# The keep factors of stick-breaking attention: a tensor_scalar on VectorE becomes an activation on ScalarE

## The chip, the core and the metric

The kernel runs on one core of a Trainium2 chip. A core has five engines that work side by side and wait for each other through semaphores: TensorE (PE, with its weight loads shown as PEld), VectorE (DVE), ScalarE (ACT), GpSimd (POOL) and SyncE (SP), which here issues the DMAs. Each engine takes its instructions in the order of its own queue. The metric is the device time of one execution in microseconds; several executions give a median.

## What is computed

A decoder trunk of two layers over 1024 tokens of width 1024, in float32. Each layer has three token mixers side by side (stick-breaking attention with 4 heads, latent attention with 4 heads, RWKV-7 with 8 heads), an output projection and a gated feed-forward part with a short convolution. What matters here is stick-breaking attention. For a query t and the positions s < t:

```python
z = einsum('bhqd,bhkd->bhqk', qb, k) * scale
past = kpos[None, :] < qpos[:, None]
log_keep = where(past, log_sigmoid(-z), 0.0)
log_later = cumsum(log_keep, axis=3, reverse=True) - log_keep
w = where(past, exp(log_sigmoid(z) + log_later), 0.0)
out = einsum('bhqk,bhkd->bhqd', w, v)
```

With T = tanh(z/2) the sigmoid of z is (1 + T)/2, and the factor 1 - sigmoid(z), the share of the stick that position s leaves over, is 0.5 - 0.5 T. So the weight of s is (1 + T_s)/2 times the product of the keep factors of all later positions. On the diagonal and behind it T is set to -1, which makes the weight 0 and the keep factor 1.

## The kernel before

Projections, RWKV and the feed-forward part make up most of the time, and in them PE is nearly always busy. The attention stage comes once per layer, at 541 to 700 us and at 2041 to 2200 us of the profiled span. In it four streams are woven together: two of latent attention (`mla`, one per head of a pair) and two of stick-breaking attention (`stick`). Each stream goes through two pairs of heads (`pr` 0 and 1) and in each through 8 blocks of 128 query rows. In pair 0 the blocks grow from 128 to 1024 key columns, in pair 1 they shrink again. So there are 32 stick-breaking blocks per layer and 64 in all, eight of each of eight lengths.

One stick-breaking block (`stick_block`, then `stick_post`) goes through these steps:

- PE multiplies queries by keys in one or two pieces of up to 512 columns (L388, L389).
- ACT takes the tangent of each piece from PSUM into the tile `be`, called `mexp` in the trace (L390).
- POOL sets the part of the last 128 columns on and above the diagonal to -1 (`affine_select`, L396).
- DVE makes the keep factors `kp` of columns 1 and up (L397), in one of three buffers called LA, T and pd in the trace.
- DVE runs the product of the keep factors from the right (a scan, L399) and multiplies by 1 + T (L400).
- PE transposes the weights in blocks of 128 (L339), ACT copies them to SBUF (L340), PE multiplies by V (L323), ACT scales the result (L418), and SP stores it.

The latent-attention streams use the same engines: DVE takes maxima (L562) and small statistics (L564, L566, L573, L576, L577), ACT the exponentials (L567, L575), DVE scales them (L580, L582). Near the end of the stage the weights of the output projection are split in two parts (L200 on ACT, L201 on DVE).

No order is written out by hand here. Semaphores are put in by the language's planner, which also orders each engine's instructions at build time, by priorities that start from the program's order and by its own estimate of when operands are ready. The engines then keep that order: an instruction whose operand is late holds up all that stand behind it on its engine.

Of the kernel before, what the change touches and what calls it, by code (L numbers as in the profile page):

```python
# [11 lines left out]
AF = mybir.ActivationFunctionType  # L12
ALU = mybir.AluOpType
# [56 lines left out]
class Body:  # L70
# [322 lines left out]
    def stick_post(self, be, kp, i, LL, nb, n, V, hp, pr, wp):  # L393
        nc = self.nc
        dg = be[:, i * P : LL]
        nc.gpsimd.affine_select(out=dg, in_=dg, pattern=[[-1, P]], base=0, channel_multiplier=1, compare_op=ALU.is_gt, fill=-1.0)  # L396
        nc.vector.tensor_scalar(kp[:, : LL - 1], be[:, 1:LL], -0.5, 0.5, op0=ALU.mult, op1=ALU.add)  # L397
        kv = kp[:, : LL - 1][:, ::-1]
        nc.vector.tensor_tensor_scan(kv, kv, self.ones.to_broadcast([P, LL - 1]), 1.0, op0=ALU.mult, op1=ALU.mult)  # L399
        nc.vector.scalar_tensor_tensor(be[:, :LL], be[:, :LL], 1.0, kp[:, :LL], op0=ALU.add, op1=ALU.mult)  # L400
        wt = self.w_transpose(self.wt4[:, n % 6], be, nb, "pa")
        self.pair(("s", pr, i), wt, hp, nb, V, self.mixd[pr], i, wp, "pa", 0.5)
# [855 lines left out]
```

## Time and profile before

| | |
|---|---|
| median of three executions | 3023.79 us (3023.44 to 3026.31) |
| the profiled execution | 3025.69 us |
| its span, first to last instruction | 3024.0 us |
| PE busy | 2913.1 us, 96% |
| PEld busy | 2322.0 us, 77% |
| DVE busy | 1727.8 us, 57% |
| ACT busy | 1074.8 us, 36% |
| POOL busy | 230.8 us, 8% |
| mean granted TensorE clock | 0.989 |

The busy times are unions of instructions of one engine within the span. A share over the whole span mixes stages in which different engines set the pace. A wait in the profile is idle time of an engine just before an instruction, put down to the instruction whose end released it.

### The profile page before, as it was taken

The numbers are of one execution on the slowest core, as the hardware profiler recorded it, in microseconds if no ns is written. First come the engines' busy times: TensorE is split into PE (matmuls) and PEld (weight loads), VectorE is DVE, ScalarE is ACT, GpSimd is POOL, SyncE is SP. The second block draws the span as 40 slices with busy tenths as digits, with TensorE's granted clock in tenths as the row PEclk, the third lists the DMA queues.
The fourth block names the chain that finished last, engine by engine and source line by source line (L and its number), as shares of the span: only waits on it lengthen the run. The fifth ranks groups of instructions, "written<-read, shape, count | busy, mean of one in ns | idle before, by whom it ended". The sixth has DMA issues, their size and how long they took to land.

```text
span 3024.0 us, 41845 instructions
## 1 busy us (share of the span) xinstructions
PE 2913.1 (96%) x16572; PEld 2322.0 (77%) x16572; DVE 1727.8 (57%) x2857; ACT 1074.8 (36%) x1833; POOL 230.8 (8%) x308
## 2 busy tenths in 40 slices
PE   8999999889999999999999999999899999999998
PEld 6777777667888888888877777776678888888887
DVE  4568665886544444344645677568965443434437
ACT  5454454762211112121254644457612111212120
POOL 0001122030000000000000011210300000000000
PEclk9999999999999999999999999999999999999999
DMA  4353666324411111111124446562244111111111
GB/s 135 91 157 102 209 193 203 92 82 137 167 56 42 42 43 55 49 56 49 63 77 125 127 133 207 177 213 66 90 145 163 42 42 42 56 49 55 50 49 56
DMA packets 338260, 301.78 MB, mean 100 GB/s; under 512 B 24200, under 2 KB 302992, under 8 KB 338064
## 3 DMA queue, kind: packets, MB, share of 16 engines
q1 hardware_dynamic: 338064, 299.11, 32.6%
q8 instruction: 131, 2.15, 0.3%
q14 instruction: 65, 0.53, 0.1%
HBM read 208.87 MB, written 90.18 MB: 99 GB/s over the span
## 4 chain that ended last, share of the span: by engine, by line
PE 76%; DVE 10%; issue 8%; ACT 3%; DMA 3%; POOL 1%; SPq 0%; POOLq 0%; DVEq 0%; ACTq 0%
PE psmm L207 16%; PE psmm L206 16%; PE psmm L205 16%; PE psps L205 5%; PE psps L206 5%; PE psps L207 5%; PE pspa L848 2%; DVE pd L731 1%; PE pspi L792 1%; PE psmt L216 1%; DMA LA<-xxd 1%; DVE T L732 1%; PE pspa L684 1%; ACT pd L726 0%; DVE mexp L400 0%
## 5 line engine op out<-in xcount | busy, mean ns | idle before, releaser
L207 PE MATMUL psmm<-xTh,wlo 128*128 128x512 f32 x2144 | 849.1, 396 | 0.0
L205 PE MATMUL psmm<-xTh,whi 128*128 128x512 f32 x2144 | 847.0, 395 | 0.0
L206 PE MATMUL psmm<-xTl,whi 128*128 128x512 f32 x2144 | 846.8, 395 | 0.0
L200 ACT CAST whi<-raw 128x1024 fp32r<-128x1024 f32 x152 | 160.0, 1053 | 1062.1 <-PE psmm L206 1048.6
L205 PEld LDWEIGHTS psmm<-xTh,whi 128*128 128x128 f32 x2144 | 404.0, 189 | 88.6 <-issue 6.1
L206 PEld LDWEIGHTS psmm<-xTl,whi 128*128 128x128 f32 x2144 | 404.2, 189 | 87.9 <-issue 4.6
L207 PEld LDWEIGHTS psmm<-xTh,wlo 128*128 128x128 f32 x2144 | 404.2, 189 | 87.6 <-issue 4.2
L201 DVE TENSOR_TENSOR wlo<-raw,whi 128x1024 fp32r<-128x1024 f32 x152 | 185.6, 1221 | 456.7 <-ACT whi L200 440.4
L1060 DVE TENSOR_TENSOR y<-y,psps 128x512 f32<-128x512 f32 x288 | 196.5, 687 | 171.1 <-PE psps L207 171.0
L205 PE MATMUL psps<-wdh,hh 128*128 128x512 f32 x672 | 266.7, 397 | 0.0
L206 PE MATMUL psps<-wdl,hh 128*128 128x512 f32 x672 | 262.9, 391 | 0.0
L207 PE MATMUL psps<-wdh,hl 128*128 128x512 f32 x672 | 259.6, 391 | 0.0
L205 PEld LDWEIGHTS psps<-wdh,hh 128*128 128x128 f32 x672 | 126.1, 188 | 36.8 <-ACT hh L200 5.9
L923 POOL TENSOR_TENSOR lsm<-lsm,small 128x1 f32<-128x1 f32 x32 | 29.3, 915 | 1629.9 <-DVE lsm L922 1629.9
L207 PEld LDWEIGHTS psps<-wdh,hl 128*128 128x128 f32 x672 | 126.2, 188 | 26.9
L206 PEld LDWEIGHTS psps<-wdl,hh 128*128 128x128 f32 x672 | 126.2, 188 | 25.4
L1035 DVE TENSOR_TENSOR cv<-cv,psmm 128x1024 f32<-128x1024 f32 x44 | 53.8, 1222 | 136.6 <-PE psmm L207 131.7
L201 DVE TENSOR_TENSOR wdl<-raw,wdh 128x1024 fp32r<-128x1024 f32 x42 | 51.5, 1226 | 88.2 <-ACT wdh L200 88.2
L1030 ACT ACTIVATE cv<-cv 128x1024 f32<-128x1024 f32 x44 | 46.7, 1061 | 115.8 <-DVE cv L1029 115.8
L848 PE MATMUL pspa<-RBl,PSl 128*128 128x128 f32 x512 | 72.0, 286 | 11.1 <-ACT QC L851 5.3
L848 PEld LDWEIGHTS pspa<-RBl,PSl 128*128 128x128 f32 x512 | 64.6, 195 | 19.3 <-ACT QC L851 8.3
L206 PE MATMUL psmm<-wol,whi 128*128 128x512 f32 x192 | 76.6, 399 | 1.6 <-DVE wol L201 1.6
(444 smaller groups left out, 4504.7 us busy)
## 6 DMA issues: line engine op xcount, KB each, us to landing
raw<-in_ffn_w_up_dram SPq DMA_DIRECT2D x88, 512.0 KB
raw<-in_w_in_dram SPq DMA_DIRECT2D x44, 512.0 KB
raw<-in_ffn_w_down_dram SPq DMA_DIRECT2D x44, 512.0 KB
rbd<-RB SPq DMA_DIRECT2D x64, 256.0 KB
PSl<-psd SPq DMA_DIRECT2D x32, 512.0 KB
RBl<-rbd SPq DMA_DIRECT2D x32, 512.0 KB
psd<-Vz SPq DMA_DIRECT2D x64, 128.0 KB
xxd<-X SPq DMA_DIRECT2D x64, 128.0 KB
```

Of the source, the lines that this page charges most:

```text
L200: self.nc.scalar.copy(hi, src)
L201: (eng or self.nc.vector).tensor_tensor(lo, src, hi.bitcast(F32), op=ALU.subtract)
L205: mm(out, lh, rh, start=start, stop=False)
L206: mm(out, lh, rl, start=False, stop=False)
L207: mm(out, ll, rh, start=False, stop=stop)
L216: nc.tensor.transpose(pt[:, k * P : k * P + P], xt[:, kk * P : kk * P + P], self.ident)
L684: ms.append(nc.tensor.matmul(pAs[h][:, cc * P : cc * P + P], flat(BK[hr, 2 * g + cc // 2, cc % 2]), AR[hr, :, 2 * g + cc // 2, cc % 2, :], ...
L731: mul = lambda o, x, y: nc.vector.tensor_tensor(o, x, y, op=ALU.mult)
L848: nc.tensor.matmul(pQ[:, f, e, :], PSh[:, f, h, e, :], RBh[:, f, h, e, :], start=True, stop=True)
L1030: nc.scalar.activation(cv, cv, AF.Gelu)
L1035: nc.vector.tensor_tensor(cv, cv, pg, op=ALU.mult)
L1060: nc.vector.tensor_tensor(y[:, i, hs], y[:, i, hs], ps, op=ALU.add)
```

## The change

The keep factors are made by ACT instead of DVE. The input, the output and the arithmetic (times -0.5, plus 0.5) are the same, and so is the place in the program: behind the clearing of the diagonal by POOL and ahead of the scan on DVE. The scan now waits for ACT instead of following an instruction of its own engine, and ACT now waits for POOL.

```diff
         dg = be[:, i * P : LL]
         nc.gpsimd.affine_select(out=dg, in_=dg, pattern=[[-1, P]], base=0, channel_multiplier=1, compare_op=ALU.is_gt, fill=-1.0)
-        nc.vector.tensor_scalar(kp[:, : LL - 1], be[:, 1:LL], -0.5, 0.5, op0=ALU.mult, op1=ALU.add)
+        nc.scalar.activation(kp[:, : LL - 1], be[:, 1:LL], AF.Copy, scale=-0.5, bias=0.5)
         kv = kp[:, : LL - 1][:, ::-1]
         nc.vector.tensor_tensor_scan(kv, kv, self.ones.to_broadcast([P, LL - 1]), 1.0, op0=ALU.mult, op1=ALU.mult)
```

## Rows read from the trace of the kernel before

**Rows 1.** The page, part 1: busy time of each engine over the span.

```profile
PE 2913.1 (96%) x16572; PEld 2322.0 (77%) x16572; DVE 1727.8 (57%) x2857; ACT 1074.8 (36%) x1833; POOL 230.8 (8%) x308
```

**Rows 2.** Busy by window: us; PE, PEld, DVE, ACT, POOL; clock, DMA share, GB/s.

```profile
541.00:590.00 49.00, 43.31 (x330) 33.33 (x330) 46.26 (x111) 38.57 (x105) 3.97 (x11) 1.00 0.33 90
590.00:632.00 42.00, 35.51 (x294) 27.85 (x293) 34.61 (x65) 28.41 (x73) 17.39 (x20) 0.94 0.15 42
632.00:690.00 58.00, 48.46 (x397) 36.43 (x395) 55.21 (x82) 38.63 (x90) 11.17 (x17) 0.97 0.28 91
...
2134.00:2193.00 59.00, 53.07 (x422) 39.39 (x420) 54.59 (x89) 39.44 (x93) 13.54 (x20) 0.99 0.32 95
```

**Rows 3.** Waits of PE, 537 to 690 and 2040 to 2197: us, times, longest.

```profile
PE pspa L339 <- DVE mexp L400: 8.3, 12, 1.5
PE psav L339 <- DVE mexp L580: 3.6, 7, 0.8
PE pspa L339 <- DVE mst L566: 3.5, 3, 2.1
...
PE psav L339 <- DVE mexp L580: 5.1, 6, 2.7
PE pspa L339 <- DVE mst L566: 2.6, 2, 2.3
PE pspa L339 <- DVE mexp L400: 2.2, 5, 0.8
```

**Rows 4.** Busy time by window, instructions of L397 alone (window, length, DVE busy).

```profile
541.00:590.00 49.00, 3.90 (x11) 1.00 0.33 90
590.00:632.00 42.00, 2.62 (x5) 0.94 0.15 42
632.00:690.00 58.00, 7.79 (x15) 0.97 0.28 91
690.00:700.00 10.00, 0.44 (x2) 0.84 0.45 125
...
2090.00:2134.00 44.00, 3.57 (x5) 0.90 0.11 34
2134.00:2193.00 59.00, 7.44 (x16) 0.99 0.32 95
```

**Rows 5.** Line L397, whole span: ns min/median/max, and idle before it.

```profile
L397 DVE TENSOR_SCALAR LA<-mexp x21: 197/479/694, 549.0 to 2191.7; 128x255 f32<-128x255 f32 x3, 128x383 f32<-128x383 f32 x3, 128x639 f32<-128x639 f32 x3, 128x767 f32<-128x767 f32 x3
...
  POOL mexp L396: 8.8, 12
```

**Rows 6.** Timeline around one cleared diagonal: start us, us, engine, line.

```profile
647.85 1.07 ACT L340 COPY Aa<-pspa 128x512 f32<-128x512 f32 x2
648.03 0.35 POOL L396 TENSOR_SCALAR_AFFINE_SELECT mexp<-mexp 128x128 f32<-128x128 f32 x1 [9.69 <-ACT mexp L390]
648.41 0.63 DVE L397 TENSOR_SCALAR T<-mexp 128x895 f32<-128x895 f32 x1 [0.18 <-POOL mexp L396]
649.08 2.02 DVE L399 TENSOR_TENSOR_SCAN T<-T,small 128x895 f32<-128x895 f32 x1
```

**Rows 7.** Lines L1030, L885, L418, L567 on ACT: ns min/median/max.

```profile
L1030 ACT ACTIVATE cv<-cv x44: 1060/1061/1062, 813.7 to 2965.8; 128x1024 f32<-128x1024 f32 x44
L885 ACT ACTIVATE yq<-ys x32: 415/417/423, 381.0 to 2024.6; 128x256 f32<-128x256 f32 x32
L418 ACT ACTIVATE avo<-pspa x32: 265/278/309, 551.3 to 2196.4; 128x128 f32<-128x128 f32 x32
L567 ACT ACT_TABLE_LOAD  x2: 1283/1283/1283, 517.4 to 2019.4; - x2
```

**Rows 8.** Timeline of DVE in stretch C of layer 0.

```profile
661.23 0.94 DVE L400 SCALAR_TENSOR_TENSOR mexp<-mexp,LA 128x768 f32<-128x768 f32 x1
...
662.16 0.55 DVE L397 TENSOR_SCALAR T<-mexp 128x767 f32<-128x767 f32 x1
...
662.83 1.74 DVE L399 TENSOR_TENSOR_SCAN T<-T,small 128x767 f32<-128x767 f32 x1
```

## Prediction

> **What bounds the kernel now.** I read the page first. TensorE (PE) is busy 96% of a span of 3024.0 us, VectorE (DVE) 57%, ScalarE (ACT) 36% [rows 1]. These are averages over stages with different limits, and the changed line runs in one stage only, the attention, once per layer. So I cut that stage out of the busy-by-window view and split each layer's copy in three: A, the first pair of heads (541 to 590 and 2041 to 2090 us), B, the turn to the second pair (590 to 632, 2090 to 2134), and C, the second pair to the end (632 to 690, 2134 to 2193) [rows 2]. The reader should compare the columns in one line. In A DVE is busy 46.3 of 49 us, PE 43.3, ACT 38.6 (A and B of layer 1 repeat those of layer 0, so only one row of each stands); in C of layer 0 it is DVE 55.2 of 58, PE 48.5, ACT 38.6; in B nobody is above 85%. So in A and C DVE is the fullest engine, at 93 to 95%, and ACT has 30% left. In B, PE, DVE and ACT take turns waiting.
>
> Whether a full DVE is also what PE waits for is a second question, answered by the waits of PE in the two stages. The three largest in layer 0 are all on DVE, 8.3 + 3.6 + 3.5 = 15.4 us, in layer 1 again, 5.1 + 2.6 + 2.2 = 9.9 us [rows 3]. Together 25.3 us: about what DVE's lateness costs PE, and a ceiling for what any relief of DVE can bring, since the work of PE stays.
>
> **What is removed.** L397 (x -> 0.5 - 0.5x, DVE) runs 64 times: 3.90 + 2.62 + 7.79 us in A, B and C of layer 0 and 0.44 us for two behind them, the same 3.9 + 3.57 + 7.44 in layer 1, in all 29.6 us [rows 4]. One takes from 0.197 us at 127 columns to 0.694 at 1023, left alone [rows 5].
>
> **What is added.** Before has no such ACT instruction, so I price it by the nearest ACTIVATEs from SBUF to SBUF with immediate or no operands: 1.061 us at 128x1024 (L1030) and 0.417 us at 128x256 (L885) [rows 7]. The line through them is 0.202 us + 0.839 ns per column. Eight of each of eight lengths, 127 to 1023, are 64 instructions and 36,800 columns: 12.9 + 30.9 = 43.8 us, 21.9 per layer. Bounds: an ACTIVATE on 128x128 from PSUM takes 0.28 us (L418) where my line says 0.31, so 2 us less is possible; the form with two operands per partition is not used, so I see no reason for more. Copies and scaled ACTIVATEs (L340, L418) run between tangents and exponentials now, and the stage has just one table load per layer (x2, 1283 ns [rows 7]), so no table load is added.
>
> The Trainium skill ("ScalarE: Activation LUTs", Rules for kernel authors) says to do additions and multiplications on VectorE and not on ScalarE. The rows agree on the single instruction: 0.69 us on DVE against about 1.06 on ACT for the longest. By that rule alone the change would lose; it is the third rival below.
>
> **What is moved: the wait for the cleared diagonal.** L397 waits for GpSimd's (POOL's) L396, which waits for the tangent L390. Before, DVE stands at this wait. It really idled there only 12 times of 64, 8.8 us in all [rows 5]; the other 52 times it came late, from other work, and the diagonal was long cleared. For those 52 the ACT version can finish before DVE wants to scan, and the DVE time simply drops out: at 662.16 L397 runs right between a product (661.23, 0.94 us) and a scan (662.83) [rows 8]. For the 12 it is the opposite. At 648.03 the diagonal is cleared in 0.35 us, L397 starts 0.03 us later and the scan follows at 649.08 [rows 6]. On ACT the same 895 columns take 0.202 + 0.751 = 0.95 us instead of 0.63, so +0.32 us; and ACT is then inside two copies that began at 647.85 and take 1.07 us, to 648.92, which is 0.54 us past the clearing [rows 6]. So such a block's scan starts 0.32 to 0.86 us later; I take 0.6. No DMA and no SP queue is passed; on POOL nothing moves. But ACT is in order: behind each new instruction stand copies of transposed weights (L340, PE's next operand), exponentials L567 (DVE's reciprocals wait for them) and tangents of the next block. Where POOL is late, all of these wait with it.
>
> **The sum, by stretch.**
> A: DVE goes from 46.3 to 42.4 us. ACT gets 11 instructions of 127 to 767 columns (4,597 in all): 2.2 + 3.9 = 6.1 us, and goes from 38.6 to 44.7 of 49. ACT becomes the fullest engine. If the stretch keeps today's 2.7 us of idle on its fullest engine, it takes 47.4: -1.6 per layer. If the longer ACT run lies wholly in the chain, +2.2 per layer (6.1 - 3.9). I take 0; bounds -3.2 and +4.4 for both layers.
> B: four of the twelve waits lie here (606, 621, 2109, 2121 us): 4 x 0.6 = +2.4. The six others give 6.2 - 2.6 = 3.6 us back to a DVE that is 82% busy, so I count half, -1.8. Sum +0.6; bounds -3.6 and +3.4.
> C: layer 0: DVE 55.2 - 7.8 = 47.4, PE 48.5, ACT 38.6 plus 15 instructions of 255 to 1023 columns (9,969 in all: 3.0 + 8.4 = 11.4 us) = 50.0. The fullest engine goes from 55.2 to 50.0. With the old 2.8 us of idle the stretch takes 52.8, -5.2; with twice that, since three engines are then within 3 us of each other and six of the twelve waits lie in the two C's, 55.6, -2.4. Layer 1: PE's 53.1 is the floor; with DVE's old idle of 4.4 us it takes 57.5, -1.5, with 2.8 us 55.9, -3.1. Both: -3.9 to -8.3. I take -5.0, nearer the small end, because the waits moved to ACT come on top.
> Sum: 0 + 0.6 - 5.0 = -4.4 us. The profiled execution took 3025.7 us, 1.7 of it outside the span, and lies 1.9 us above the median of the runs, 3023.8. I set the change against the median: 3023.8 - 4.4 = **3019.4 us**. Everything outside the two stages (2706 of 3024 us) should be as before, apart from small shifts of order at their edges.
>
> **Rivals.**
> 1. Full relief. For it: PE's largest waits are on DVE, and 52 of 64 factors are not urgent. Then PE wins back half of its 25.3 us of waits on DVE, -12.7 us: 3011. Against it: PE, DVE and ACT would all be at 85 to 90%, and ACT feeds PE too.
> 2. Nothing passes. ACT takes DVE's place as the late engine in A, and in C PE's in-order transposes keep the pace: 3022 to 3026. For it: ACT at 44.7 of 49 in A. Against: C has room on ACT.
> 3. Slower: ACT's queue becomes the bound. Place: A, and the twelve blocks where the diagonal is only just cleared. Price: +4.4 in A, and 12 x 0.6 = 7.2 for the late scans, with no relief used: +11.6, 3035. It decides from the point where ACT, not DVE, is what PE's transposes and score products wait for; ACT's 6.1 us more in A must then displace copies rather than fill its 10.4 us of idle. For it: each factor is 1.5 times as long on ACT, and ACT's idle pieces in A are short. Against: its free time there is larger than what is added.
> 4. The change does not do what it says: the planner places the new instruction late on ACT, or orders PE otherwise, and the stage moves by some us either way.
>
> **How the numbers follow.** A measurement of this kernel tells about 0.2%, 6 us, from no change. Forecast (-10 to +1): 0.40, of which 0.16 lies beyond -6. Rival 1: 0.20, all faster. Rival 2: 0.15, of which 0.02 slower. Rival 3: 0.23, of which 0.03 stays within 6 us. Rival 4: 0.02, half faster, half slower. Faster 0.16 + 0.20 + 0.01 = 0.37; same 0.24 + 0.13 + 0.03 = 0.40; slower 0.02 + 0.20 + 0.01 = 0.23. The range runs from 3006 (rival 1 with two thirds of the ceiling) to 3034 (most of rival 3). The likeliest case alone: 3014 to 3025.
>
> **What would show it.** Right: L397 on ACT at about 0.31 to 1.06 us, 43 to 44 us in all; DVE busy 14 to 15 us less per layer; PE's waits on DVE's L400 and L580 shorter; C of layer 0 shorter by some 3 us, A unchanged; no new table load. Rival 3: ACT idle before L397 <- POOL well over 8.8 us, and PE's top waits on L340, L567 or L390. Rival 1: both C's shorter by 4 us or more and A shorter too. I would be wrong above all if a different order on PE moved the stage by more than the terms above.

## The result and the profile after

The changed kernel takes 3040.67 us (median of four runs, 3037.40 to 3046.96), the kernel before on the same chip 3024.61 (3023.44 to 3026.31): a ratio of 1.0055, interval 1.0038 to 1.0073. It is slower by 16 us, where the forecast was 4.4 us faster and the range ended at 3034. The profiled execution took 3046.96 us with a span of 3045.2, so it lies 6.3 us above the median; the table of its span is read with that in mind.

The page of the changed kernel, part 1, beside [rows 1]:

```profile
PE 2923.0 (96%) x16572; PEld 2331.3 (77%) x16572; DVE 1706.8 (56%) x2793; ACT 1111.0 (36%) x1897; POOL 228.9 (8%) x308
```

The 64 instructions have moved from DVE to ACT. The number of products is the same, and yet TensorE (PE) is busy for 2923.0 us where it was busy for 2913.1, and idle for 3045.2 - 2923.0 = 122.2 us where it was idle for 3024.0 - 2913.1 = 110.9. So of the 21.2 us between the two spans 11.3 are waits and 9.9 are longer products.

Busy time by window in the changed kernel, with the windows and columns of [rows 2] (PE, PEld, DVE, ACT, POOL; clock, DMA share, GB/s). The second layer's stage ends some 21 us later (its last L397 starts at 2213.7 us, row below, that of before at 2192.6), so a row no longer holds quite the same blocks:

```profile
541.00:590.00 49.00, 43.91 (x322) 33.91 (x321) 42.12 (x95) 41.02 (x109) 4.97 (x11) 0.93 0.32 87
590.00:632.00 42.00, 35.83 (x305) 27.54 (x303) 33.73 (x67) 33.16 (x85) 10.01 (x12) 1.00 0.09 24
632.00:690.00 58.00, 45.78 (x353) 36.78 (x354) 39.50 (x55) 40.04 (x88) 17.24 (x22) 0.85 0.31 93
...
2134.00:2193.00 59.00, 46.37 (x363) 37.14 (x360) 42.09 (x62) 42.14 (x92) 19.37 (x25) 0.88 0.25 72
```

Look at the third and fourth rows, stretch C. Neither DVE nor ACT is full any more (39.5 and 40.0 of 58 us, where DVE had 55.2); all three engines wait for one another. PE gets through 353 products where it did 397, at a granted clock of 0.85 where it was 0.97 (layer 1: 0.88 where it was 0.99), so more of the stretch was at the lower of the two levels, 1.2 GHz.

The waits of PE in the changed kernel, 541 to 700 us and, below the dots, 2041 to 2193, beside [rows 3] (us, times, longest):

```profile
PE pssc L205 <- ACT mexp L567: 6.6, 7, 3.0
PE pspa L339 <- DVE mexp L400: 4.1, 7, 1.2
PE pspy L389 <- POOL kl L373: 3.9, 1, 3.9
PE psav L339 <- DVE mexp L580: 2.9, 5, 1.5
PE pspq L388 <- POOL qh L373: 1.9, 1, 1.9
...
PE pssc L205 <- ACT mexp L567: 6.9, 7, 3.3
PE pspa L339 <- DVE mexp L400: 6.7, 8, 1.3
PE pspq L389 <- POOL kl L373: 2.2, 2, 1.4
```

The wait for L400 in layer 0 has halved, 8.3 to 4.1 us, as the relief of DVE should do; in layer 1 it has grown, 2.2 to 6.7. At the top now stand exponentials on ACT (L567), and there is a new wait for the low parts of the second pair's queries and keys, which POOL makes (L373). Each query and key is split in two: ACT casts it to a rounded part (L362, L363), and the low part is what the rounding left over, the source minus the cast; PE multiplies with both.

The new instruction itself, line L397 over the whole span, beside [rows 5] (ns min/median/max; idle before it; who waited for it):

```profile
L397 ACT ACTIVATE T<-mexp x22: 309/648/1078, 543.5 to 2213.7; 128x127 f32<-128x127 f32 x4, 128x511 f32<-128x511 f32 x4, 128x895 f32<-128x895 f32 x4, 128x255 f32<-128x255 f32 x2
...
  POOL mexp L396: 10.7, 17
...
  DVE T L399: 8.4, 6
  DVE pd L399: 6.4, 5
```

It takes 0.31 to 1.08 us, as priced. ACT stands at the cleared diagonal 17 times for 10.7 us, and scans on DVE wait for the factors.

How the second pair begins is worth a closer look. The timeline of the changed kernel in layer 0 (start, us, engine, line; in brackets the idle time before and what ended it), one answer per engine:

```profile
629.57 0.40 PE L388 MATMUL pspy<-kh,qh 128*128 128x512 f32 x1
630.38 0.50 PE L389 MATMUL pspq<-kl,qh 128*128 128x512 f32 x1 [0.41 <-POOL kl L373]
634.79 0.80 PE L389 MATMUL pspy<-kl,qh 128*128 128x512 f32 x1 [3.91 <-POOL kl L373]
...
627.76 1.06 ACT L363 CAST kh<-pst 128x1024 fp32r<-128x1024 f32 x1
...
624.80 3.47 POOL L373 TENSOR_TENSOR qh<-pst,qh 64x256 fp32r<-64x256 f32 x4 [4.27 <-ACT qh L362]
...
628.90 5.83 POOL L373 TENSOR_TENSOR kl<-pst,kh 128x256 fp32r<-128x256 f32 x4 [0.26 <-ACT kh L363]
```

PE reaches the first product with the keys' low parts at 630; POOL can begin them only at 628.90, when ACT has cast the keys (627.76), and needs 5.83 us for the four pieces; PE stands for 3.91 us. The two casts of keys in this stretch, first of the kernel before and then of the changed one (line L363, 612 to 652 us):

```profile
L363 ACT CAST kh<-pst x2: 1045/1050/1056, 614.1 to 623.6; 128x1024 fp32r<-128x1024 f32 x2
```

```profile
L363 ACT CAST kh<-pst x2: 1058/1062/1067, 627.8 to 642.5; 128x1024 fp32r<-128x1024 f32 x2
```

They begin 13.7 and 18.9 us later. Those casts and low parts are not touched by the edit. What moved them is the planner: with one instruction on another engine it wrote a new order, and of the 13,948 places of PE's list alone 1,472 hold another instruction than in the old order (the lists written out in the kernels of e16 and e1).

### The profile page after: what moved, and what is told of

It is laid out like the page before. It is cut to its first block, busy times and chain, and to the rows that moved or that the text cites. A ratio compares the mean times of both kernels' runs of the same rounds, so it can differ in the third digit from the quotient of the medians.

```text
span 3045.2 us, 41788 instructions
## 1 busy us (share of the span) xinstructions
PE 2923.0 (96%) x16572; PEld 2331.3 (77%) x16572; DVE 1706.8 (56%) x2793; ACT 1111.0 (36%) x1897; POOL 228.9 (8%) x308
## 4 chain that ended last, share of the span: by engine, by line
PE 75%; DVE 9%; issue 8%; ACT 3%; DMA 3%; POOL 1%; SPq 0%; DVEq 0%; POOLq 0%; ACTq 0%
PE psmm L207 16%; PE psmm L205 16%; PE psmm L206 16%; PE psps L205 5%; PE psps L206 5%; PE psps L207 5%; DVE pd L731 2%; PE pspa L848 1%; PE pspi L792 1%; PE psmt L216 1%; DVE T L732 1%; DMA LA<-xxd 1%; PE pspa L684 1%; ACT pd L726 0%; PE pspy L875 0%
## 5 line engine op out<-in xcount | busy, mean ns | idle before, releaser
L1030 ACT ACTIVATE cv<-cv 128x1024 f32<-128x1024 f32 x44 | 46.7, 1061 | 116.1 <-DVE cv L1029 116.1
```

Of the source, the lines that this page charges most:

```text
L1030: nc.scalar.activation(cv, cv, AF.Gelu)
```

## The experiments

Two things changed at once, then: the engine that makes the factor, and the order of everything around it. The theories: **A** or **Q**, ScalarE's queue (44 us more of work in front of casts, copies and exponentials); **D** and **W**, the wait (ScalarE stands at the cleared diagonal, the scans stand behind it); **O**, the planner's new order, whatever the factor does; **P**, within that, the second pair's casts and low parts. In some kernels every engine's list is fixed by hand, one order edge from each instruction to the next; the edit is then

```diff
         Body(ctx, tc, a).run()
+        pin(tc)   # every engine: each instruction behind the one before it in a given list
```

| kernel | order | factor made on | median us | ratio to before (interval) |
|---|---|---|---|---|
| changed | planned | ScalarE | 3040.7 | 1.0055 (1.0038 to 1.0073) |
| e1 | of before | ScalarE | 3036.8 | 1.0043 (1.0030 to 1.0055) |
| e2 | of changed | VectorE | 3055.6 | 1.0106 (1.0092 to 1.0120) |
| e3, low parts on VectorE | planned | ScalarE | 3017.0 | 0.9979 (0.9970 to 0.9988) |
| e4, low parts on VectorE | planned | VectorE | 3020.1 | 0.9989 (0.9980 to 0.9999) |
| e7, low parts on VectorE | of e4 | ScalarE | 3035.7 | 1.0039 (1.0028 to 1.0051) |
| e5, load only | of before | VectorE | 3026.7 | 1.0006 (0.9998 to 1.0015) |
| e5b, load and wait | of before | VectorE | 3033.7 | 1.0027 (1.0015 to 1.0039) |
| e6, 15 stay | of before | 49 ScalarE, 15 VectorE | 3039.1 | 1.0045 (1.0033 to 1.0057) |
| e10, divided | of before | both | 3028.7 | 1.0015 (1.0007 to 1.0024) |
| e11, divided | planned | both | 3022.8 | 0.9993 (0.9985 to 1.0002) |
| e12, divided | of changed | both | 3044.9 | 1.0063 (1.0050 to 1.0077) |
| e14, diagonal first | planned | ScalarE | 3022.8 | 0.9985 (0.9977 to 0.9994) |
| e16, casts moved | of changed | ScalarE | 3036.1 | 1.0039 (1.0025 to 1.0053) |
| e17, divided, casts moved | of changed | both | 3040.8 | 1.0053 (1.0041 to 1.0066) |
| e9, low parts on VectorE, divided | planned | both | 3016.6 | 0.9972 (0.9961 to 0.9983) |
| e8, low parts on VectorE, diagonal first | planned | ScalarE | 3015.2 | 0.9971 (0.9959 to 0.9982) |
| e13, the same | planned | VectorE | 3014.6 | 0.9965 (0.9952 to 0.9977) |
| e15, the same | planned | both | 3011.6 | 0.9951 (0.9939 to 0.9964) |

**Engine and order apart.** e1 is the changed kernel in the order of before; e2 the kernel before in the order of the changed one.

> The keep factors on ACT, but the issue order of every engine is that of the kernel before, written down by hand; only the 64 keep factors leave DVE's list and stand in ACT's list where ACT came free after the diagonal had been cleared in the trace of before. Theory O (the 16 us come from the new order that the planner chose): with the old order the change is worth what the sum by stretches gave, 3017 to 3024 us. Theory A (ACT's queue is the price: longer factors, copies and exponentials behind them): still slower than before, 3032 to 3042 us.

> The keep factors on DVE as in the kernel before, each right ahead of its scan, but the issue order of every engine is that of the changed kernel. Theory O: the order alone is bad, 3037 to 3050 us, more than the changed kernel because DVE carries its 29.6 us again. Theory A: without the factors on ACT the loss is gone, 3020 to 3029 us.

e1 came to 3036.8 and e2 to 3055.6. Each part loses by itself: the engine 13 us in the old order, and the new order 31 us with the factor on VectorE, 15 of which the factor on ScalarE gives back (e2 lies above both ranges). With the factor on ScalarE the two orders lie only 4 us apart, e1 and the changed kernel, and their intervals do not tell that from nothing. So neither theory alone is right, and a warning lies in the pair: an order written for one placement costs 13 us (e1) or 15 us (e2 against the changed kernel) when the factor is put in the other. A fixed order is a harsh test of either.

**ScalarE's queue, taken to pieces in the old order.** e5 keeps VectorE's factors and adds the same 64 instructions to ScalarE, reading a constant; in e5b they read the cleared tile:

```diff
         nc.vector.tensor_scalar(kp[:, : LL - 1], be[:, 1:LL], -0.5, 0.5, op0=ALU.mult, op1=ALU.add)
+        nc.scalar.activation(self.idle[:, : LL - 1], self.ones.to_broadcast([P, LL - 1]), AF.Copy, scale=-0.5, bias=0.5)   # e5
+        nc.scalar.activation(self.idle[:, : LL - 1], be[:, 1:LL], AF.Copy, scale=-0.5, bias=0.5)                           # e5b
```

> The kernel before with its own order of instructions on every engine, VectorE still making the keep factors, and beside that 64 extra ScalarE instructions of the same form and lengths, in the places that they have in the old order with the factors on ScalarE. They read a constant, wait for nothing and nobody uses their result, so this is ScalarE's 44 us alone, without the wait for the cleared diagonal and without VectorE's relief. Theory Q (the 44 us themselves, standing ahead of ScalarE's casts and copies, cost the time): 3034 to 3045 us, as much as the old order with the factors on ScalarE (3037) or more. Theory D (what costs is that ScalarE stands at the clearing and the scans come later): 3022 to 3028.

> As the run with the load alone, but the 64 extra instructions read the tile with the cleared diagonal, so that ScalarE also stands at the clearing; VectorE still makes the factors that are used, so no scan waits for ScalarE (the later product in place on the tile does). Theory Q: within 4 us of the load alone, 3034 to 3045. Theory D in its first half (ScalarE standing at the clearing holds up what is queued behind it): 3034 or more here and 3022 to 3028 with the load alone; in its second half (the scans that come later): both near 3024.

> The old order with the factors on ScalarE, but the 15 blocks in which VectorE had nothing else to do when the clearing ended (by the trace of before) keep theirs on VectorE. Theory D: those 15 made the loss, so 3022 to 3028, at least 8 us less than with all 64 on ScalarE (3037). Theory Q: the loss goes with the load, so about three quarters of it stay, 3032 to 3037.

The load alone costs 2 us, within the 0.2% that can be told; theory Q falls for this order. With the wait it costs 9 (the profiled execution of e5b, 3038.3 us, is the slowest of its six). Line L398, the added instruction, in e5b (what ended ScalarE's idle time before it), then PE's wait for ScalarE's copies of transposed weights, 515 to 735 us, in e5 and in e5b:

```profile
L398 ACT ACTIVATE idle<-mexp x64: 308/685/1068, 542.1 to 2204.6; 128x127 f32<-128x127 f32 x8, 128x255 f32<-128x255 f32 x8, 128x383 f32<-128x383 f32 x8, 128x511 f32<-128x511 f32 x8
...
  POOL mexp L396: 17.2, 24
```

```profile
PE pspa L323 <- ACT Aa L340: 2.6, 4, 1.4
```

```profile
PE pspa L323 <- ACT Aa L340: 5.2, 5, 2.1
```

ScalarE stands 24 times, 17.2 us, and what PE pays for the copies queued behind doubles. VectorE's product in place (L401 in e5b), which has to wait for the added reading of its tile, is not what pays: it has no idle time before it. The Trainium skill ("PSUM — Partial Sum Buffer", Engine vs sequencer instructions) says it in five words, "ScalarE/VectorE/GpSimdE queues are strict FIFO"; the trace agrees. In e1 the scans wait besides. Its factor line:

```profile
  POOL mexp L396: 17.3, 25
...
  DVE T L399: 8.8, 5
  DVE pd L399: 8.5, 9
  DVE LA L399: 6.6, 6
```

That is 23.9 us of waiting on DVE for factors, and no gain of the relief is left: e1 lies 3 us above e5b, which has no relief at all (by the ratios, 5). But the blocks that I had called the dear ones are not: with the 15 of them on VectorE for which VectorE had nothing else to do when the clearing ended (e6; my twelve are those with an idle time of DVE charged to the clearing), the time stays, 3039, above both ranges.

**The wait taken away.** In e10 to e12 each factor is divided at the diagonal block, and ScalarE makes only what needs no clearing:

```diff
-        nc.scalar.activation(kp[:, : LL - 1], be[:, 1:LL], AF.Copy, scale=-0.5, bias=0.5)
+        d0 = max(i * P - 1, 0)
+        nc.vector.tensor_scalar(kp[:, d0 : LL - 1], be[:, d0 + 1 : LL], -0.5, 0.5, op0=ALU.mult, op1=ALU.add)
+        if i:
+            nc.scalar.activation(kp[:, :d0], be[:, 1 : d0 + 1], AF.Copy, scale=-0.5, bias=0.5)
```

> The old order with the factors on ScalarE, but ScalarE makes only the columns left of the diagonal block, which need nothing from GpSimd, in the same places of its list as before; the last 127 or 128 columns, which need the clearing, stay on VectorE in the factors' old place (56 ScalarE and 64 short VectorE instructions). Theory W (the loss is the wait: ScalarE stands at the clearing with its copies and exponentials behind it, and the scans stand behind ScalarE): 3015 to 3027 us, at least 10 below the old order with whole factors on ScalarE (3037). Theory L (long factors on ScalarE cost it, waiting or not): 3033 to 3040.

> The changed kernel with the same division of each factor (left of the diagonal on ScalarE, the diagonal's columns on VectorE), the planner free to order it. Theory W: 3018 to 3032 us, 9 to 22 below the changed kernel (3041); theory O (the planner's new order with its late low parts on GpSimd is the loss): 3036 to 3046.

> Every engine in the order of the changed kernel, but each factor divided: ScalarE makes the columns left of the diagonal, which wait for nothing of GpSimd, in the factor's place of its list; VectorE makes the diagonal's columns right ahead of the scan. Theory W (the loss is the wait at the clearing): 3020 to 3032 us, 9 or more below the changed kernel (3041). Theory O (the new order is bad in itself): 3036 to 3055, between the changed kernel and the same order with whole factors on VectorE (3056).

In the old order 8 of the 13 us go (e10, 3028.7, between the ranges of the two theories). With the planner free the whole loss goes (e11, 3022.8). That looked like proof of theory W until e12: the changed kernel's own order without ScalarE's wait takes 3044.9, no less than with it. e11 and e12 are the same program and differ in the order alone, by 22 us, so the division helps in e11 only together with the order that the planner wrote for it. e12 does not show that the wait costs nothing, for the wait has moved. What ended VectorE's idle time before its short piece (L398) in e12:

```profile
  POOL mexp L396: 8.6, 3
```

VectorE now stands at the clearing, once for 5.9 us, and has 64 instructions back, in an order that was written without them. (In e11 it stands there longer, 14.0 us, 9 times, in a fast kernel.) The waits of PE in e12, 541 to 700 us, show the second pair's low parts in their place, though no factor on ScalarE waits for POOL:

```profile
PE pspy L389 <- POOL kl L373: 2.9, 1, 2.9
PE pspq L388 <- POOL qh L373: 1.9, 1, 1.9
```

e14 shortens the wait in another manner, by making the piece of the scores with the diagonal first in the wide blocks:

```diff
-        for u, (a0, a1) in enumerate(self.pieces(LL)):
+        for u, (a0, a1) in enumerate(self.pieces(LL)[::-1]):
```

> The changed kernel, and in blocks wider than 512 columns (32 of 64) the piece of the scores with the diagonal is made first, so that the clearing runs beside the other piece's tangent; the low parts stay on GpSimd. Theory W: 3024 to 3034 us, since the wide blocks' waits go. Theory O: 3036 to 3046.

3022.8, and ScalarE's idle time at the clearing falls from 10.7 us, 17 times, to

```profile
  POOL mexp L396: 4.2, 6
```

The planner ordered this kernel anew, too, so e14 does not say whether the shorter wait or the new order took the 18 us.

**What in the order.** In e3, e4, e7 VectorE makes the second pair's low parts in one piece, and POOL is out of that chain:

```diff
-SPLIT_STICK = (0, 4)
+SPLIT_STICK = (0, 0)
```

> The changed kernel with the low parts of queries and keys of the second pair of heads made on DVE in one piece each instead of on POOL in four. In the changed kernel PE stands 3.9 + 1.9 + 0.4 us for these in layer 0 and 1.4 + 0.8 + 0.9 in layer 1, and its clock falls to half behind that. If the late split on POOL is what the change cost: 3024 to 3030 us. If it is not: within 4 us of 3040.7, since DVE gets 4 x 2 x 1.2 us of work per layer pair and POOL's waits only move.

> Control for the run with the changed kernel: the kernel before with the same splits on DVE. There PE waited for none of POOL's splits by more than 0.4 us, so nothing is won and DVE, the full engine, gets some 5 to 10 us more per layer: 3026 to 3040 us.

> The order of the kernel before with the second pair's low parts on VectorE in one piece (3020 us) on every engine, and the factors on ScalarE in that order. Theory P (the loss goes by way of ScalarE's casts of the second pair's queries and keys to GpSimd's four-piece low parts, for which TensorE waits): within 4 us of its control, 3016 to 3024, as with the planner's own order (3017). Theory Q (ScalarE's queue anyway): 3028 to 3035, the +13 us of the first old-order run again.

Both are faster than was expected of them. With the planner free the change is now worth -3 us (3017.0 against 3020.1, with intervals that overlap) where it was +16. In a fixed order it costs 15.6 us once more (e7 against e4), with POOL out of the chain, so the fixed-order loss is not that chain's. e16 and e17 keep the changed kernel's order and move eight casts in ScalarE's list, to stand right behind the last tangent that reads the first pair's products:

```diff
 L390 ACTIVATE mexp_6170<-pspy_6175 128x512
+L362 CAST qh_1093_6315<-pst_6309 128x1024
+L363 CAST kh_1094_6316<-pst_6310 128x1024
 ...
 L567 ACTIVATE mexp_6198,mst_6197<-pssc_6199,mst_6197 128x384
-L362 CAST qh_1093_6315<-pst_6309 128x1024
```

> The changed kernel in its own order on every engine, save the second pair's eight casts of queries and keys on ScalarE: they stand directly behind the tangent of the last product that reads the first pair's (by the changed kernel's trace 4 to 15 us earlier), so that GpSimd makes the low parts earlier. Theory P (in the new order the late casts, and GpSimd behind them, hold up TensorE and let its clock fall): 3024 to 3034 us, since TensorE's waits for these parts were 10 us and the low clock behind them comes on top. Theory O (the new order is slow through and through): 3036 to 3044.

> The same moved casts in the changed kernel's order with divided factors (3045 without the move). Theory P: 3024 to 3036 us. Theory O: 3038 to 3048.

Both come 4 to 5 us down (3040.7 to 3036.1 and 3044.9 to 3040.8), so theory P's ranges are missed and theory O's are met; in each pair the intervals of the ratios overlap, and the size is no more than an estimate. In e16 the casts of keys begin at 617.7 and 627.7 us, and of PE's waits from 541 to 700 us that for the keys' low parts falls from 3.9 us to

```profile
PE pspy L389 <- POOL kl L373: 0.9, 1, 0.9
```

Its page has PE busy for 2914.7 us instead of 2923.0, so the products are shorter again too. That profiled execution (span 3028.8) lies at the low end of its runs, 3030.5 to 3037.4, so its sizes are not to be set against the median. By the medians the late casts would be about a quarter to a third of the 16 us.

**The best version, and its control.** e8 and e9 set one cure each on top of e3, e13 is e8 with the factor on VectorE, and e15 has all three edits.

> The changed kernel with the second pair's low parts on VectorE and, in blocks wider than 512 columns, the piece of the scores that holds the diagonal first, so that the clearing runs beside the other piece's tangent. Control as in the run before, 3017 us. Theory W: 3008 to 3016 us, most of ScalarE's idle before the factors (8 us) gone in the wide blocks; theory O: 3014 to 3026, some us either way with another order.

> As the run before, and the second pair's low parts on VectorE in one piece. Its control is the changed kernel with those low parts on VectorE (3017 us). Theory W: 3006 to 3016 us, since the last ScalarE waits for the clearing (8 us of idle, 16 times) go; theory O: 3014 to 3022, nothing left to gain once the order is good.

> Control: factors on VectorE, the second pair's low parts on VectorE, the diagonal's piece first. Theory W: VectorE hardly waited for the clearing, so within 3 us of the same kernel with the pieces in their old order (3020): 3017 to 3023. If the planner's luck with the order made the gain of the run with the changed kernel (3015), it is as fast here: 3012 to 3016.

> All three together: low parts on VectorE, diagonal's piece first, factors divided. Theory W: either of the last two takes the wait away, so no better than each alone by more than 3 us: 3011 to 3017.

e15 has the lowest median, 3011.6 us, 0.49% under the kernel before, though its interval overlaps those of e8, e9 and e13. But the control speaks against the change: with low parts and pieces as in e8, the factor on VectorE takes 3014.6 and on ScalarE 3015.2, no difference that can be told. And in e8 ScalarE still stands at the clearing for 8.4 us, 15 times:

```profile
  POOL mexp L396: 8.4, 15
```

not much less than the 10.7 us of the changed kernel, which is 25 us slower. A wait of that size is paid or not paid according to what stands around it.

## Why the prediction was wrong, point by point

**The single prices were right.** The removed and the added instructions are there at their lengths (0.31 to 1.08 us), and no table load was added. The load on ScalarE by itself costs about what the sum gave it in stretch A, nothing (e5, +2 us). The Trainium skill's rule to multiply and add on VectorE ("ScalarE: Activation LUTs", Rules for kernel authors) agrees with the trace for the single instruction and does not decide the time: e8 and e13, whose sources differ in that alone, cannot be told apart.

**The first step that failed is the one that held the rest still.** The sum was made on the old order: "Everything outside the two stages (2706 of 3024 us) should be as before, apart from small shifts of order at their edges", and the planner's order was the fourth rival with 0.02 and "some us either way". The planner wrote another order, and for one and the same program an order is worth far more than that: 31 us with the factors on VectorE (e2 against the kernel before), 22 us with divided factors (e12 against e11). With whole factors on ScalarE, the case that was predicted, the old order and the new one are both slow, 3037 and 3041 us (e1 and the changed kernel), so the 16 us are not simply the price of the new order over the old one. Nor are they the price of the instruction: with the low parts on VectorE the planner found orders in which the same factors on ScalarE cost nothing (e3, e8). I had named another order as what would make me wrong above all, and priced it at nearly nothing. The rows had a warning that I did not use: POOL's 17.4 us in B [rows 2] are mostly the low parts of the second pair (15.7 us by the same window for L373 alone), which share POOL with the cleared diagonals, and their casts share ScalarE with the new instruction. Three queues are tied together at that turn, where I counted only late scans.

**The second is a term that was left at nothing: what is queued behind ScalarE's stops.** For the sum fails in the old order, too. There the change costs 13 us, not -4.4. Term by term: the load 0 (measured +2); the wait, in B four late scans of 0.6, +2.4, and for the C's only a smaller relief (measured about 7 in all as e5b less e5, from the 24 stops of ScalarE and what is queued behind them; keeping 15 late scans on VectorE gave nothing back, e6); the relief in C, -5.0 (no gain shows: e1 lies above e5b). The prediction said that where POOL is late all that is queued behind the new instruction waits with it, and then gave that no number: what pays is not the scan of that block but ScalarE's next copies and exponentials. The third rival had this, "ACT's queue becomes the bound", and its 3035 is close to e1's 3036.8, in part by luck: it was added up from the load in A (+4.4, where the whole load measured +2) and from late scans (+7.2), not from the queue behind the stops.

**Its signs in the profile were mixed.** ACT's idle time before the factor rose only from the 8.8 us that DVE had [rows 5] to 10.7; PE's top wait did become L567. Of the signs for the forecast the shorter wait for L400 came in layer 0 alone; DVE's busy time fell by 21.0 us, where 28 to 30 had been foretold; C did not become shorter.

**The lower clock was in no case.** In the profiled executions, of the 21.2 us between the spans 9.9 are longer products. Busy time by window in the changed kernel, behind the stop at 630.88 us (3.91 us) and behind one at 654.40 (2.96 us, for L567):

```profile
633.20:639.80 6.60, 5.01 (x29) 4.25 (x30) 2.26 (x5) 2.41 (x5) 1.83 (x2) 0.50 0.24 89
657.10:663.70 6.60, 6.35 (x38) 5.85 (x40) 6.60 (x10) 5.05 (x12) 1.20 (x2) 0.50 0.00 0
```

In both the granted clock is 0.50, the lower level of 1.2 GHz, while PE is busy for 5.0 and 6.4 of 6.6 us. The kernel before has such stretches too, but fewer: its C of layer 0 is at 0.97 in the mean, this one at 0.85. The prediction priced a stop of PE at its length alone. That the stops bring the lower clock on is argued from their order in time; no run held the stops and changed the clock. And it is not every stop: e1 has one of 2.8 us at 626 us, and its stretch from 590 to 632 us has a granted clock of 1.00. The page of e1, part 1:

```profile
PE 2913.5 (96%) x16572; PEld 2322.0 (77%) x16572; DVE 1704.8 (56%) x2793; ACT 1108.8 (37%) x1897; POOL 233.0 (8%) x308
```

Its span is 3035.2 us, so PE is idle for 121.7 us, as in the changed kernel (122.2), but busy no longer than before. In these two executions the factors on ScalarE come with about 11 us more of waiting in either order, and the longer products with the new one alone.

**What stays open.** How the 16 us divide between the new order and what is queued behind ScalarE's stops is not settled: the stops were measured alone in the old order only, and the new order alone with the factors on VectorE only. The late casts are some 4 to 5 us by the medians. For the rest, some 11 us, moved low parts, later exponentials and the clock stand side by side in the trace, and no run took them apart. Nor can the runs say whether the planner had to come to a bad order with this change or happened to: the change was worth +16, -3 and +0.6 us in the three pairs of planned kernels whose sources differ in nothing else (changed and before, e3 and e4, e8 and e13); the last two are within what can be told.

## What to carry to other kernels

Where a planner writes the order, an edit to one instruction is a draw of a new order: give that its own share of the range before terms of 5 us are added up (here one program moved by 22 us and another by 31 of some 3024 with the order alone), and test the edit in more than one surrounding. To learn what an edit costs in itself, divide it on the chip into load, wait and relief (a dummy instruction that reads a constant, then one that reads the awaited tile); a fixed old order is no neutral ground, since it was written for one placement: here the other cost 13 to 15 us more in it. And before an instruction that waits for a slow engine is moved to a queue, list what stands behind it there: in the old order that was about 7 us.

## What the runs showed that was not expected

An instruction of 0.3 to 1.1 us, 64 times on ScalarE, cost PE almost nothing as long as it waited for nothing (44 us of work, +2 us), and 9 us when it waited 17.2 us in all. A ScalarE wait of 8 to 11 us at the clearing stood in kernels of 3015 (e8) and 3041 us. And in C of layer 0 the granted clock was 0.85 where it had been 0.97, for the same kind of products: with stops of PE of 2 to 4 us ahead of the stretches at the lower level, nearly half of the time lost between the profiled executions (9.9 of 21.2 us) is longer products.
